# Layer 1's delta-rule scan in a fixed TensorE order: steps of three and six heads, outputs gated straight from PSUM

## The chip, the core and the metric

The kernel runs on one core of one Trainium2 chip. Its time is device microseconds (us) of one execution, the median of several runs. Below, TensorE (PE in the views) does the matmuls and PEld its weight loads, VectorE is DVE, ScalarE is ACT, GpSimd is POOL, and SP issues most DMAs.

## What is computed

A decoder of two layers over 512 tokens of width 1024, in fp32. The first layer mixes tokens with six heads of a gated delta rule, the second with sliding-window attention; both also attend to 256 memory tokens, and both end in a projection `w_out`, a residual add and a SwiGLU block. The change lies in the first layer's scan and what follows it:

```python
def step(state, inp):
    u_n, w_n, a_n, qg_n, kg_n, gl_n = inp
    v_new = u_n - jnp.einsum("bhck,bhkv->bhcv", w_n, state)
    o_n = jnp.einsum("bhck,bhkv->bhcv", qg_n, state) + jnp.einsum("bhcs,bhsv->bhcv", a_n, v_new)
    state = state * gl_n[..., None, None] + jnp.einsum("bhck,bhcv->bhkv", kg_n, v_new)
    return state, o_n
...
o = rms_norm(o, norm_g) * jax.nn.silu(z.reshape(b_sz, s_len, GDN_HEADS, GDN_DV).astype(jnp.float32))
...
x = x + jnp.concatenate([mix_out.astype(x.dtype), mem_o.astype(x.dtype)], axis=-1) @ w_out[layer]
```

## The kernel before, in words

Everything lies feature-major: a tile holds 128 features by 512 tokens. Big products run in fp32r with both operands split into a high and a low part (`mm3`, L205): three matmuls of 128x512 for each 128 features, so a projection (`project`, L213) is 24 of them. A weight arrives by DMA as `wraw` (L183); ScalarE makes its high part `whi` and VectorE its low part `wlo` (`split`, L175). `whi` and `wlo` have three buffers each.

The scan works in chunks of 128 tokens, four for each of the six heads, in plain fp32 products of 128x128. `scan_step` (L726) does one head and one chunk, in five products, called here by what they make:

- the *state* product, from `kn` and the state `S`; VectorE makes `R` of it;
- the *solve* product, from `Tt` and `R`; ScalarE copies it out as `v` (tile `vn`);
- the *keys* product, from `v` and `kg`; VectorE makes the new `S` of it (not in the last chunk);
- the *past* product (`gcr` and the old `S`) and the *own* product (`v` and `DT`), which add up to the chunk's output; ScalarE copies it into `qg` (tile `gcr`).

A head's first chunk has no state: `R` is the value tile itself and the state and past products are left out. All five products of one step lie in one PSUM bank, `sc`, of which there are three; three banks `pj` serve projections and two banks `g` the rest. The value tile (tile `N`) is made from a projection of the input (`conv_tile`, L465: ScalarE's copy, then three taps on VectorE, tile `qv`), a SiLU on ScalarE, four transposes on TensorE into a bank `g`, and one VectorE product.

`gdn` (L475) calls values of heads 0 to 2, their chunks 0 to 2, values of heads 3 to 5, chunk 3 of heads 0 to 2, all chunks of heads 3 to 5, and `finish` (L629), which squares the output, adds the stored square of `q`, sums over features with a matmul by ones (`g<-N,ones`), takes Ln and Exp on ScalarE, multiplies by the norm's gain and by the gate (the stored SiLU of `z`, loaded into `kg`), and splits the result for `output` (L872), whose eight rows of `w_out` each take 24 matmuls. The calls' order is not the order on an engine: a scheduler puts each engine's instructions in an order of its own, within what depends on what, and so mixes products of the scan with those of the value projections and of the first rows of `w_out`. Each engine then runs its list strictly in that order.

## Time and profile before

| | us |
|---|---|
| median of 3 runs (1147.73 to 1148.5) | 1147.86 |
| the profiled execution | 1147.79 |
| its span, first to last instruction | 1146.0 |
| TensorE busy | 1125.1 (98%) |
| VectorE busy | 841.2 (73%) |
| ScalarE busy | 632.8 (55%) |
| mean granted TensorE clock | 0.998 |

Times in the views count from the span's start. An fp32 matmul shows as two records, since it is done in two passes. A matmul's record is longer than the time until the next one can start, so a busy TensorE need not be a TensorE at its peak; start-to-start times tell more. The layer's scan and `finish` lie between about 206 and 280 us.

### The profile page before, as it was taken

What the parts mean: (1) busy time and instruction counts of PE and PEld (TensorE: products, weight loads), DVE (VectorE), ACT (ScalarE), POOL (GpSimd) and SP (SyncE); (2) the same over time, 40 slices, a digit from 0 to 9 for tenths busy, and PEclk for the clock granted to TensorE, in tenths of its full rate; (3) what the DMA queues carried; (4) which work ended last, traced back from release to release, by engine and by line L of the source; (5) the groups of instructions that cost most, each with busy time, mean ns of one, the idle gap of its engine ahead of it and who ended that gap; (6) DMA issues with size and microseconds to landing.
All of it is one profiled execution on the core that took longest, in us unless ns stands there. A gap on an engine that the chain in (4) does not pass through costs nothing.

```text
span 1146.0 us, 19675 instructions
## 1 busy us (share of the span) xinstructions
PE 1125.1 (98%) x7476; PEld 990.9 (86%) x7476; DVE 841.2 (73%) x1591; ACT 632.8 (55%) x1274; POOL 86.0 (8%) x97
## 2 busy tenths in 40 slices
PE   7999999999999999999999999999999999999996
PEld 6888877887899998899998777777999988999986
DVE  6754887766789987489866777859699843898754
ACT  7669572366566652256654556855566522566533
POOL 0310000000101100011100000010011100111000
PEclk9999999999999999999999999999999999999999
DMA  8433342324667744567723411244477733577232
GB/s 310 148 92 115 117 109 96 100 85 166 171 151 187 185 126 126 150 153 188 175 73 102 138 57 56 65 102 129 107 187 187 191 108 106 141 192 185 70 96 93
DMA packets 73971, 152.76 MB, mean 133 GB/s; under 512 B 17756, under 2 KB 18420, under 8 KB 73876
## 3 DMA queue, kind: packets, MB, share of 16 engines
q1 hardware_dynamic: 62356, 130.52, 36.9%
q0 software_dynamic: 11520, 20.98, 11.5%
q8 instruction: 59, 0.97, 0.4%
q14 instruction: 36, 0.29, 0.1%
HBM read 144.51 MB, written 6.96 MB: 132 GB/s over the span
## 4 chain that ended last, share of the span: by engine, by line
PE 84%; DVE 8%; ACT 3%; DMA 2%; issue 1%; SPq 0%; DVEq 0%; ACTq 0%
PE pj L153 39%; PE g L153 37%; PE sc L153 6%; DVE wlo L160 2%; ACT sm L141 2%; ACT whi L147 1%; PE qk L153 1%; DMA wraw<-in_wout 1%; DVE btmp L160 1%; DVE l L163 1%; PE pt L157 1%; DVE big L160 1%; DMA wraw<-in_wmk 1%; PE g L157 1%; DVE stats L791 0%
## 5 line engine op out<-in xcount | busy, mean ns | idle before, releaser
L147 ACT ACTIVATE whi<-wraw 128x512 fp32r<-128x512 f32 (+2 forms) x331 | 244.1, 746 | 238.3 <-PE pj L153 150.5
L160 DVE TENSOR_TENSOR wlo<-wraw,whi 128x512 fp32r<-128x512 f32 (+2 forms) x331 | 274.2, 838 | 100.4 <-ACT whi L147 94.7
L153 PE MATMUL pj<-h,whi 128*128 128x512 f32 (+1 forms) x676 | 265.5, 394 | 0.0
L153 PE MATMUL pj<-l,whi 128*128 128x512 f32 (+1 forms) x676 | 263.9, 390 | 0.4 <-DVE l L163 0.4
L153 PE MATMUL pj<-h,wlo 128*128 128x512 f32 (+1 forms) x676 | 263.6, 390 | 0.0
L153 PE MATMUL g<-T,whi 128*128 128x256 f32 x1280 | 228.1, 278 | 0.2
L153 PEld LDWEIGHTS g<-T,whi 128*128 128x128 f32 x1280 | 194.7, 188 | 1.8 <-DVE fu L163 1.8
L153 PE MATMUL g<-T,wlo 128*128 128x256 f32 x640 | 177.8, 278 | 0.0
L153 PEld LDWEIGHTS pj<-h,whi 128*128 128x128 f32 x676 | 126.8, 188 | 29.0 <-issue 3.3
L153 PEld LDWEIGHTS pj<-h,wlo 128*128 128x128 f32 x676 | 127.0, 188 | 25.9 <-DVE wlo L160 0.4
L153 PEld LDWEIGHTS pj<-l,whi 128*128 128x128 f32 x676 | 127.1, 188 | 25.7 <-DVE l L163 0.8
L153 PE MATMUL g<-h,whi 128*128 128x256 f32 (+1 forms) x508 | 144.4, 284 | 0.0
L153 PE MATMUL g<-h,wlo 128*128 128x256 f32 (+1 forms) x508 | 144.2, 284 | 0.0
L153 PE MATMUL g<-l,whi 128*128 128x256 f32 (+1 forms) x508 | 144.2, 284 | 0.0
L153 PEld LDWEIGHTS g<-T,wlo 128*128 128x128 f32 x640 | 120.1, 188 | 0.0
L153 PEld LDWEIGHTS g<-l,whi 128*128 128x128 f32 x508 | 95.3, 188 | 1.2
L153 PEld LDWEIGHTS g<-h,whi 128*128 128x128 f32 x508 | 95.3, 188 | 1.2
L153 PEld LDWEIGHTS g<-h,wlo 128*128 128x128 f32 x508 | 95.3, 188 | 1.1
L1046 POOL DMA_DIRECT2D ws<-in_wgu x40 | 35.8, 894 | 709.6 <-DMA ws<-in_wgu 313.9
L147 ACT ACTIVATE whi<-ws 128x512 fp32r<-128x512 f32 x80 | 50.5, 631 | 49.0 <-PE g L153 40.1
L160 DVE TENSOR_TENSOR fu<-pj,rstd 128x512 f32<-128x512 f32 (+1 forms) x34 | 22.4, 660 | 54.5 <-PE pj L153 54.5
L160 DVE TENSOR_TENSOR wlo<-ws,whi 128x512 fp32r<-128x512 f32 x80 | 54.9, 686 | 6.4 <-ACT whi L147 6.3
(372 smaller groups left out, 1622.0 us busy)
## 6 DMA issues: line engine op xcount, KB each, us to landing
wraw<-in_wgu SPq DMA_DIRECT2D x48, 512.0 KB, 4.2
ws<-in_wgu SPq DMA_DIRECT2D x80, 256.0 KB, 3.4
ws<-in_wgu POOLq DMA_DIRECT2D x80, 256.0 KB, 4.9
wraw<-in_wdn SPq DMA_DIRECT2D x48, 384.0 KB, 3.1
wraw<-in_win SPq DMA_DIRECT2D x26, 512.0 KB, 3.6
wraw<-in_wgu SPq DMA_DIRECT2D x40, 256.0 KB, 4.5
wraw<-in_wout SPq DMA_DIRECT2D x16, 512.0 KB, 3.5
wraw<-in_wdn SPq DMA_DIRECT2D x16, 256.0 KB, 2.7
```

The source lines that it names most:

```text
L141: ins = self.nc.scalar.activation(out, in_, func, **kw).ins
L147: self.copied = self.nc.scalar.activation(out, in_, AF.Copy, **kw).ins
L153: return self.nc.tensor.matmul(out, lhsT, rhs, start=start, stop=stop, skip_group_check=more).ins
L157: return self.nc.tensor.transpose(out, in_, self.ident[:k, :k]).ins
L160: return eng.tensor_tensor(out=out, in0=a, in1=b, op=op).ins
L163: self.nc.vector.scalar_tensor_tensor(out=out, in0=in0, scalar=scalar, in1=in1, op0=op0, op1=op1)
L1046: nc.gpsimd.dma_start(s1, a22, accum_op=ALU.add)
```

## The change

The scan is rewritten, and TensorE's order in it is fixed: between `lock(True)` and `lock(False)` every matmul and transpose gets an order dependency on the one before it, so that TensorE's list there is the order of the calls. VectorE's and ScalarE's lists are still the scheduler's. In detail:

- Values of heads 0 to 3 are projected first, then heads 0 to 2 are turned and take chunk 0; then come the projections of heads 4 and 5, the turning of heads 3 and 4, chunk 1 of heads 0 to 2, and the turning of head 5.
- Heads 0 to 2 then do chunks 2 and 3 together with chunks 0 and 1 of heads 3 to 5 (six heads in a step); heads 3 to 5 do chunks 2 and 3 by themselves. No other matmul stands inside a step. Between the last two steps stand the sums by ones of heads 0 to 2.
- In a step of three heads the output goes to a bank of its own (`g` or `pj`); in one of six it stays in the step's bank. It is squared by ScalarE from PSUM (into `N`) and multiplied by the gate by VectorE from PSUM (into `gcr`), chunk by chunk. The gates are loaded ahead, into the tiles `big` and `X64`. The copy of the output, the later squares and the later gate products go.
- For heads 3 to 5 the sum by ones takes its input in high and low fp32r parts. Rows 0 to 2 of `w_out` are done k by k, the three rows in turn.

Of the code (line numbers differ between the two kernels):

```diff
+    def chained(self, ins):
+        if self.locked:
+            if self.latest is not None:
+                self.nosync(ins, self.latest)
+            self.latest = ins
+        return ins
...
+        def scan(*steps):
...
+            run("state", todo)
+            if len(groups) > 1:
+                run("solved", todo)
+                for three in groups:
+                    run("keys", three)
+                    for s in three:
+                        s["past"]()
+                        s["own"]()
+                return
+            run("past", todo[:1])
+            run("solved", todo)
+            run("past", todo[1:])
+            run("keys", todo)
+            run("own", todo)
...
-        values(first)
-        scan(first, range(NC - 1))
-        values(second)
-        scan(first, range(NC - 1, NC))
+        self.lock(True)
+        vs += [values(2), values(3)]
+        for h in first:
+            turn(h)
+        scan(*alone(first, 0))
+        vs += [values(4), values(5)]
+        turn(3)
+        turn(4)
+        scan(*alone(first, 1))
+        turn(5)
         self.use(LN_EXP)
-        scan(second)
+        scan(*beside(first, 2, "sc"), *beside(second, 0, "pj"))
+        scan(*beside(first, 3, "sc"), *beside(second, 1, "pj"))
+        squares(first, False)
+        scan(*alone(second, 2))
+        total(first, "pj")
+        scan(*alone(second, 3))
         finish(first)
+        squares(second, True)
...
-        self.mm(ps[:, 2, :], v, AT[:, c, :], S is None, True)
-        self.copy(qg[:, c, :], ps[:, 2, :])
+        def own():
+            self.mm(po, t["v"], AT[:, c, :], old is None, True)
+            self.square(vt[:, c, :], po)
+            self.tt(nc.vector, qg[:, c, :], po, gate[:, c, :], ALU.mult)
```

Three places show what the order becomes; the numbers behind a name tell buffers apart.

**The first chunk.** TensorE before, where heads 0 and 1 start their first chunk (`sc<-N,Tt` is the solve product, `sc<-vn,kg` the keys product, `pj` a value projection):

```order
L157 MATMUL g_2226<-consts_66,qv_2146 128x128 x4
L153 MATMUL sc_2238<-N_572,Tt_1422 128x128
L153 MATMUL pj_2350<-h_456,whi_2346 128x512
L153 MATMUL pj_2350<-l_457,whi_2346 128x512
L153 MATMUL pj_2350<-h_456,wlo_2347 128x512
L153 MATMUL sc_2247<-N_572,Tt_1422 128x128
L153 MATMUL pj_2350<-h_461,whi_2346 128x512
L153 MATMUL pj_2350<-l_462,whi_2346 128x512
L153 MATMUL sc_2238<-vn_2240,kg_131_653 128x128
L153 MATMUL sc_2247<-vn_2249,kg_142_705 128x128
```

TensorE now, the whole first step:

```order
L168 MATMUL g_2265<-consts_66,qv_2109 128x128 x4
L168 MATMUL g_2271<-consts_66,qv_2146 128x128 x4
L168 MATMUL g_2277<-consts_66,qv_2191 128x128 x4
L154 MATMUL sc_2283<-N_572,Tt_1422 128x128
L154 MATMUL sc_2285<-N_572,Tt_1422 128x128
L154 MATMUL sc_2287<-N_572,Tt_1422 128x128
L154 MATMUL sc_2283<-vn_2290,kg_131_653 128x128
L154 MATMUL sc_2285<-vn_2293,kg_142_705 128x128
L154 MATMUL sc_2287<-vn_2296,kg_153_757 128x128
L154 MATMUL g_2284<-DT_112_559,vn_2290 128x128
L154 MATMUL g_2286<-DT_113_560,vn_2293 128x128
L154 MATMUL pj_2288<-DT_114_561,vn_2296 128x128
```

The projections that stood between the products stand ahead of them and behind them. VectorE now, at the same place (`wlo_2742` is the low part of row 0 of `w_out`, `qv_2228` head 3's value):

```order
L171 TENSOR_TENSOR N_572<-g_2265,f_890 128x512
L171 TENSOR_TENSOR N_572<-g_2271,f_890 128x512
L171 TENSOR_TENSOR wlo_2742<-wraw_2739,whi_2741 128x1024
L174 SCALAR_TENSOR_TENSOR qv_2228<-pj_2235,gains_67,qv_2228 128x511
L171 TENSOR_TENSOR N_572<-g_2277,f_890 128x512
```

Head 2's value product stands behind a weight part and a tap.

**The second chunk of heads 0 to 2.** VectorE now (`qv_2353` is head 5's value, three taps; `R` follows the state products):

```order
L171 TENSOR_TENSOR N_572<-g_2390,f_890 128x512
L171 TENSOR_TENSOR N_572<-g_2396,f_890 128x512
L174 SCALAR_TENSOR_TENSOR qv_2353<-pj_2360,gains_67,qv_2353 128x511
L174 SCALAR_TENSOR_TENSOR R_2409<-sc_2402,negc_536,N_572 128x128
L174 SCALAR_TENSOR_TENSOR qv_2353<-pj_2360,gains_67,qv_2353 128x510
L174 SCALAR_TENSOR_TENSOR R_2412<-sc_2404,negc_536,N_572 128x128
L174 SCALAR_TENSOR_TENSOR qv_2353<-pj_2360,gains_67,qv_2353 128x509
L174 SCALAR_TENSOR_TENSOR R_2415<-sc_2406,negc_536,N_572 128x128
L171 TENSOR_TENSOR wlo_2768<-wraw_2765,whi_2767 128x1024
L174 SCALAR_TENSOR_TENSOR S_2430<-S_2299,egl_539,sc_2402 128x128
```

ScalarE at the same place:

```order
L148 ACTIVATE whi_2767<-wraw_2765 128x1024
L148 ACTIVATE qv_2353<-pj_2360,gains_67 128x512
L148 ACTIVATE vn_2419<-sc_2402,f_890 128x128
L148 ACTIVATE vn_2422<-sc_2404,f_890 128x128
L142 ACTIVATE qv_2353<-qv_2353 128x512
L133 ACT_TABLE_LOAD
L148 ACTIVATE vn_2425<-sc_2406,f_890 128x128
```

The three R alternate with the taps of a projection that ends just before; the third `v` stands behind that value's SiLU and the load of the table for Ln and Exp. Before, VectorE alternated R and taps in the same way at one place (R_2474, R_2484, R_2494), with rows of `w_out` between the products on TensorE.

**From the second step of six to chunk 2 of heads 3 to 5.** VectorE now (`gcr<-pj` and `gcr<-sc` are the gate products, `N<-N,kg` the sums of heads 0 to 2):

```order
L174 SCALAR_TENSOR_TENSOR S_2581<-S_2509,egl_539,pj_2529 128x128
L174 SCALAR_TENSOR_TENSOR S_2584<-S_2512,egl_539,pj_2530 128x128
L174 SCALAR_TENSOR_TENSOR S_2587<-S_2515,egl_539,pj_2531 128x128
L171 TENSOR_TENSOR N_572<-N_572,kg_493_2604 128x512
L171 TENSOR_TENSOR gcr_109_550<-pj_2529,big_2183 128x128
L171 TENSOR_TENSOR gcr_110_551<-pj_2530,X_396_2188 128x128
L171 TENSOR_TENSOR N_572<-N_572,kg_494_2607 128x512
L171 TENSOR_TENSOR gcr_111_552<-pj_2531,X_396_2188 128x128
L174 SCALAR_TENSOR_TENSOR R_2617<-sc_2610,negc_536,N_572 128x128
```

The first R of the next step has the gate products and the sums of the step before it in front of it.

184 lines of the change are left out of this document (115 added, 69 removed).

## Prediction

> **What bounds the kernel now.** The page first: busy times, and the chain that ended last by engine.
>
> ```profile
> PE 1125.1 (98%) x7476; PEld 990.9 (86%) x7476; DVE 841.2 (73%) x1591; ACT 632.8 (55%) x1274; POOL 86.0 (8%) x97
> PE 84%; DVE 8%; ACT 3%; DMA 2%; issue 1%; SPq 0%; DVEq 0%; ACTq 0%
> ```
>
> TensorE sets the time, so a microsecond that it waits in the scan is a microsecond of the kernel. Whether it waits there isn't seen in "busy"; it is counted from start-to-start times. The windows by stage for the scan and its finish, whole and for tile `sc` alone, then two groups of that window:
>
> ```profile
> 206.00:280.00 74.00, 72.74 (x413) 59.26 (x412) 50.52 (x92) 42.21 (x92) 0.00 (x0) 1.00 0.37 113
> 206.00:280.00 74.00, 30.50 (x204) 27.58 (x204) 11.34 (x36) 14.13 (x48) 1.00 0.37 113
> L157 PE MATMUL g<-consts,qv 128*128 128x128 f32 x24 | 3.6, 273 | 0.0
> L153 PE MATMUL g<-N,ones 128*128 128x512 f32 x12 | 6.1, 610 | 1.0 <-DVE N L160 1.0
> ```
>
> So 228 records of 128x128 (204 and 24), 12 sums by ones, and 173 others of 128x512. Their spacing, from the chain (72 matmuls), and from the timeline:
>
> ```profile
> 313.00 16.34 PE pj L153 x72
> 219.86 0.53 PEld L153 LDWEIGHTS sc<-S,kn 128*128 128x128 f32 x4
> 220.31 0.19 PEld L153 LDWEIGHTS pj<-h,whi 128*128 128x128 f32 x1
> 251.81 1.02 PE L153 MATMUL g<-N,ones 128*128 128x512 f32 x2
> 252.67 0.38 PE L153 MATMUL sc<-vn,kg 128*128 128x128 f32 x2
> ```
>
> A 128x512 takes 16.34/72 = 0.227 us; four records of 128x128 take 0.45, so 0.1125 each and 0.225 for a scan product; two records by ones take 0.86. The window's work is 173 x 0.227 + 228 x 0.1125 + 6 x 0.86 = 70.1 us of 74: **TensorE waits only 3.9 us there**, because projections stand between the dependent products. That is all that a better order could win.
>
> How long a link of the scan takes, on the timeline of two heads (loads, VectorE, ScalarE, in order of time):
>
> ```profile
> 220.40 0.61 DVE L163 SCALAR_TENSOR_TENSOR R<-sc,negc,N 128x128 f32<-128x128 f32 x2 [0.81 <-PE sc L153]
> 220.81 0.55 PEld L153 LDWEIGHTS sc<-R,Tt 128*128 128x128 f32 x4
> 221.40 0.62 ACT L147 ACTIVATE vn<-sc,f 128x128 f32<-128x128 f32 x2 [0.86 <-PE sc L153]
> 221.82 0.56 PEld L153 LDWEIGHTS sc<-vn,kg 128*128 128x128 f32 x4
> 222.35 0.60 DVE L163 SCALAR_TENSOR_TENSOR S<-S,egl,sc 128x128 f32<-128x128 f32 x2 [0.94 <-PE sc L153]
> 222.75 0.32 PEld L153 LDWEIGHTS sc<-gcr,S 128*128 128x128 f32 x2
> ```
>
> From a product's load to its reader 0.54 (219.86 to 220.40; 0.53 and 0.59 for the others); each R, `v` or S 0.31; from its end to the next load 0.10. So state to solve is 0.95 us, solve to keys 1.01, keys to state 0.93: a ring of 2.9 us, against 15 products x 0.225 = 3.4 us in a step of three heads. By this ring alone such a step has no gap. What decides is whether VectorE and ScalarE start their parts at once; with both lists run strictly in order, that is read from what stands ahead. The durations:
>
> ```profile
> L160 DVE TENSOR_TENSOR wlo<-wraw,whi 128x1024 fp32r<-128x1024 f32 x9 | 11.0, 1217 | 1.7 <-ACT whi L147 1.7
> L147 ACT ACTIVATE whi<-wraw 128x1024 fp32r<-128x1024 f32 x7 | 7.3, 1056 | 4.4 <-PE pj L153 2.4 <-DMA wraw<-in_win 2.0
> L163 DVE SCALAR_TENSOR_TENSOR qv<-pj,gains,qv 128x511 f32<-128x511 f32 x5 | 3.7, 746 | 0.4 <-ACT qv L147 0.4
> L160 DVE TENSOR_TENSOR N<-g,f 128x512 f32<-128x512 f32 x6 | 4.1, 691 | 6.9 <-PE g L157 6.9
> L160 DVE TENSOR_TENSOR N<-N,kn 128x512 f32<-128x512 f32 x6 | 4.0, 688 | 3.4 <-DMA kn<-q 3.4
> L141 ACT ACTIVATE qv<-qv 128x512 f32<-128x512 f32 x6 | 3.8, 627 | 3.7 <-DVE qv L163 3.5
> L132 ACT ACT_TABLE_LOAD x1 | 1.3, 1283 | 0.0
> L147 ACT ACTIVATE gcr<-sc 128x128 f32<-128x128 f32 x24 | 6.5, 275 | 8.8 <-PE sc L153 8.5
> 212.07 0.59 PEld L157 LDWEIGHTS g<-consts,qv 128*128 128x128 f32 x4
> 212.93 0.69 DVE L160 TENSOR_TENSOR N<-g,f 128x512 f32<-128x512 f32 x1 [0.73 <-PE g L157]
> ```
>
> **The change, part by part.** *TensorE's work.* The scan's products are the same. Heads 3 to 5 sum by two fp32r matmuls (0.454) in place of 0.86: 3 x 0.41 = **1.2 us less**.
>
> *Work moved between VectorE and ScalarE.* 24 copies (0.275), six squares and six gate products go; 24 squares and 24 gate products of 128x128 come, three splits too. In sum it costs nothing: the busy sums are 50.5 and 42.2 of 74 us, and VectorE gains about 5 (24 x 0.30 and three splits of 0.69, less six gate products of 0.69). No row shows the new pieces: I take 0.28 for a square (like the copy, the nearest) and 0.30 for a gate product (half of the paired S's 0.60, also two operands, one from PSUM); 0.27 to 0.37 holds both. Nothing is gained on the path, as the copies were off it: no product reads the output. In the new lists VectorE's gate product waits for ScalarE's square of the same bank, so an output is out 0.54 + 0.28 + 0.30 after its own product's load.
>
> *Six gate loads*, ahead of head 4's weights on SP's queue, the first of them waiting for the triangular solve's last reading of `X64`. The rows of the DMA issues (count, size, median us to landing) that bear on this and on the end:
>
> ```profile
> wraw<-in_win SPq DMA_DIRECT2D x26, 512.0 KB, 3.6
> x<-in_xT SPq DMA_DIRECT2D x8, 256.0 KB, 4.1
> kg<-z SPq DMA_DIRECT2D x6, 256.0 KB, 2.9
> ```
>
> Heads 2 and 3 (48 x 0.227 = 10.9 us) are projected meanwhile, so I put it at nothing; were that cover gone, the weight would come 3.6 late, or later by as much as it shares the queues with the gates.
>
> *The first chunk*, time from the end of head 3's projection. A turn's N starts 0.86 after its load (212.07 to 212.93). N0 runs 0.86-1.55, N1 to 2.24; then `wlo` to 3.46 and a tap to 4.20 stand ahead of N2, which ends at 4.89. So head 2's solve product loads at 4.99, its `v` ends at 5.84, its keys product starts at 5.94, and the step's last product ends at 6.8. The work is 12 x 0.1125 + 9 x 0.225 = 3.4: **3.4 us of waiting**.
>
> *The second chunk.* N3 and N4 end at 2.24; tap, R, tap, R, tap, R: the R's end at 3.28, 4.33 and 5.37 where the state products were ready by 2.1. Solve products load at 3.4, 4.4 and 5.5. The third `v` stands behind the SiLU (tap's end 5.07, so to 5.9) and the table load (to 7.2): it ends at 7.5, the keys product follows at 7.6, the step ends at 8.5. Work 0.9 + 15 x 0.225 = 4.3: **4.2 us**. Before, the table load and the taps were there too, with projections to fill the time; now nothing else may pass.
>
> *First step of six.* Head 5's turn needs a bank `g` that the gate product of the step before frees: own product at 7.82, square to 8.64, gate to 8.97, turn at 9.07, N5 to 10.62, then R0, so the first solve product loads at 11.03 in place of 9.6: 1.4. Past and own products share the bank with the keys product here, so they wait until S is read out of it: 0.3 for head 0's and 0.7 in sum for heads 3 to 5's. **2.4 us**.
>
> *Second step of six.* The state products of heads 3 to 5 wait for gate products to free their banks `pj`, and R's run at 0.31 against products at 0.225: the last solve product is 0.5 late. Then head 3's past product waits some 1.0 for S, which stands behind three gate products and a sum (0.69) on VectorE. 27 products are 6.1, and I count 7.5: **1.4 us**.
>
> *Chunk 2 of heads 3 to 5.* Ahead of its R's stand, from the last S, two sums (0.69) and three gate products: 2 x 0.69 + 3 x 0.30 = 2.3. The state product loads 0.8 after that S, and its R could start at 1.35: 0.95 late, and 1.1 with the spacing of the R's: **1.1 us**.
>
> *Chunk 3.* ScalarE's list has three Ln, two Exp and a high part of the first heads ahead of its `v`:
>
> ```profile
> L141 ACT ACTIVATE N<-g,eps 128x512 f32<-128x512 f32 x6 | 4.1, 687 | 1.9 <-PE g L153 1.9
> L147 ACT ACTIVATE h<-gcr 128x512 fp32r<-128x512 f32 x6 | 3.8, 630 | 2.4 <-DVE gcr L160 2.3
> L141 ACT ACTIVATE N<-N 128x512 f32<-128x512 f32 x6 | 3.8, 629 | 0.0
> ```
>
> 3 x 0.69 + 2 x 0.63 + 0.63 = 4.0, from some 1.2 after the first sum loads: 5.2. The first `v` could start when three sums (2.6), three state products and a past one (0.9) and a solve's 0.54 are over, with 0.1 of R: 4.1. **1.1 us**.
>
> *Rows 0 to 2* end together, k by k. Row 3's `whi` waits for row 0's buffer (1.06), its `wlo` (1.22) stands behind two residual adds (0.69 each): about 2.9 after row 1's end against four or five matmuls that can run; and `x` is loaded after the last norm product and lands 4.1 later, which is no later than row 0 is summed. With smaller waits in the second sums: **2.2 us**, from 1 to 3.
>
> Sum: 3.4 + 4.2 + 2.4 + 1.4 + 1.1 + 1.1 + 2.2 = 15.8 us of new waits; less the 3.9 of now, less 1.2 of work: **+10.7 us**. The profiled execution took 1147.79 (span 1146.0 and 1.8 around it; the median is 1147.86): **1158.5 us**.
>
> A rule on the banks bears on the gate products. In the row of 222.75, `sc<-gcr,S` reads the old state alone, yet loads 0.10 after the first S has been read from its bank (222.35 + 0.30): engines take turns at a bank. The Trainium skill ("PSUM — Partial Sum Buffer", PSUM bank collisions raise a hardware error) says that the scheduler does so for any two engines, two readers too. Were square and gate product at once, each boundary would be 0.3 shorter, the sum about 1 us less.
>
> **The rivals.** *Only the first two chunks cost.* If the later steps wait no more than the kernel does now: +3.4 + 4.2 - 1.2 - 2.0 (half of the 3.9, for half of the window) = +4.4: 1152.2. For it: the ring of 2.9 in a step of 3.4. Against it: the gate products ahead of the R's.
>
> *Faster: the ring decides.* If N2 and the R's come in time, no step has a gap and TensorE gets back all: -3.9 - 1.2 = 1142.7; it decides where the R's stand at most 0.5 us behind their state products (3.4 less 2.9). For it: 98% busy and VectorE at 50.5 of 74. Against it: the lists above, with a `wlo` and three taps in front.
>
> *A slower clock after the waits.* At the start, after 7 us with nothing to do, TensorE takes nearly twice as long for a 128x256 (the waits' row, then four matmuls):
>
> ```profile
> PE pj L153 <- ACT whi L147: 7.1, 1, 7.1
> 10.72 0.41 PE L153 MATMUL pj<-mh,whi 128*128 128x256 f32 x1
> 10.93 0.41 PE L153 MATMUL pj<-ml,whi 128*128 128x256 f32 x1
> 11.90 0.28 PE L153 MATMUL pj<-ml,whi 128*128 128x256 f32 x1
> 12.02 0.28 PE L153 MATMUL pj<-mh,wlo 128*128 128x256 f32 x1
> ```
>
> That is 0.21 apart, then 0.12; the change comes some 4 us after the wait's end. The first step holds one wait of 2.7 us (from 2.3 to 4.99), the second four of 0.8 to 1.5. If such waits slow TensorE for as long as the start did, each of the two steps adds 2: 1162.5. Against it: shorter, and the window's clock is 1.00 with waits in it. The Trainium skill ("TensorE: Matmul & The Clock Gate", Why this matters for your kernels) asks for no idle gaps over about 3 us; by it the wait just passes. *Nothing happens*: 1147.8, if the new waits are a third of what I count.
>
> **How the numbers follow.** Forecast 0.65; first chunks alone 0.15; slower clock 0.07; faster 0.08; no change 0.05. The likeliest: 1158.5. Its own ends are 1154 (no tail, and half of what I count from the first step of six on) and 1162.5 (pieces of 0.37, a tail of 3, S and R at 0.35 as singles). With the second case, 1151 to 1163 holds about 0.8. Slower by over 0.2% (2.3 us, about what a measurement of this kernel can tell) 0.87, within 0.05, faster 0.08.
>
> **What would show it.** Right: between the projections of heads 3 and 4 some 6.8 us in place of 3.4, `N<-g` behind `wlo` at its end; R's spaced 1.05 in the second step, `vn` behind the table load; the scan and its finish some 10 us longer, all else the same. Wrong: steps of three that take 3.4 us from first to last load, or a `wlo` that has long run when N1 ends.

## The result, and the profile after

The change makes the kernel slower: 1155.28 us, the median of 6 executions from 1154.77 to 1157.57, against 1147.8 for the kernel before, measured beside it. The ratio is 1.0071 [1.0058, 1.0084], or +7.5 us. A second set, taken later, gave 1156.77 against 1147.55, 1.0074 [1.006, 1.0087], +9.2. The forecast was 1158.5, +10.7: slower, as forecast, and by waits of the kind that were forecast, but 3.2 less than that.

The page of the kernel after, busy times and the chain by engine:

```profile
PE 1127.3 (98%) x7476; PEld 994.8 (86%) x7476; DVE 844.3 (73%) x1612; ACT 631.6 (55%) x1271; POOL 86.3 (7%) x97
PE 88%; DVE 6%; ACT 3%; DMA 1%; issue 1%; SPq 0%; DVEq 0%; ACTq 0%
```

The profiled execution took 1155.4 with a span of 1153.6, 7.6 more than before. TensorE's share of the chain rises from 84 to 88% and VectorE's falls from 8 to 6, while the scan holds more waits: the chain's shares do not show where the time goes. The busy sum does not either; at a halved clock a matmul also counts as busy for longer.

The windows by stage, over the same stretch as before (PE, PEld, DVE, ACT, POOL busy, the granted clock, the DMAs):

```profile
206.00:280.00 74.00, 67.69 (x384) 57.38 (x383) 50.12 (x108) 37.67 (x85) 0.00 (x0) 0.98 0.25 81
```

TensorE has 384 records in place of 413 there, is idle for 6.3 us in place of 1.3, and its clock is 0.98 in place of 1.00. Two things, then: waits, and a slower clock. What TensorE waited for between 190 and 300 us (total, times, longest):

```profile
PE sc L154 <- DVE R L174: 2.6, 5, 1.0
PE sc L154 <- DVE N L171: 1.2, 1, 1.2
PE g L168 <- ACT qv L142: 1.0, 1, 1.0
PE sc L154 <- ACT vn L148: 0.9, 1, 0.9
PE pj L154 <- DVE S L174: 0.4, 1, 0.4
PE g L168 <- DVE gcr L171: 0.2, 1, 0.2
```

And the same view of the kernel before, from 200 to 290 us:

```profile
PE g L153 <- DVE N L160: 1.0, 1, 1.0
PE sc L153 <- ACT gcr L147: 0.3, 1, 0.3
```

The waits are 6.3 us against 1.3. They are on the tiles that the forecast named, `N`, `R`, `v` (tile `vn`), `S` and, for turn 5, the gate products (`gcr`); only `qv`, a SiLU, is new. The first step's place, on the timeline after:

```profile
216.45 1.03 PEld L168 LDWEIGHTS g<-consts,qv 128*128 128x128 f32 x8
216.68 1.03 PE L168 MATMUL g<-consts,qv 128*128 128x128 f32 x8
218.52 1.22 DVE L171 TENSOR_TENSOR wlo<-wraw,whi 128x1024 fp32r<-128x1024 f32 x1
218.75 0.66 PE L168 MATMUL g<-consts,qv 128*128 128x128 f32 x4 [1.04 <-ACT qv L142]
219.66 0.74 DVE L174 SCALAR_TENSOR_TENSOR qv<-pj,gains,qv 128x511 f32<-128x511 f32 x1
220.32 0.68 DVE L171 TENSOR_TENSOR N<-g,f 128x512 f32<-128x512 f32 x1
221.05 0.65 PE L154 MATMUL sc<-N,Tt 128*128 128x128 f32 x2 [1.20 <-DVE N L171]
222.78 1.06 PE L154 MATMUL g<-DT,vn 128*128 128x128 f32 x4
223.92 0.77 PE L154 MATMUL pj<-h,whi 128*128 128x512 f32 x1
```

From the first turn to head 4's projection are 7.24 us, of which 3.4 is work. Head 2's turn waits for its SiLU; its `N` stands behind `wlo` and a tap as forecast; and four records of an own product then take 1.06 where four took 0.61 elsewhere (the row of 242.53, the same product in the second chunk). That is the clock, for 3.4 us, in the windows of the last section.

The second chunk, where the list on VectorE alternates taps and R's, and ScalarE has the table load:

```profile
235.25 1.04 PE L168 MATMUL g<-consts,qv 128*128 128x128 f32 x8
238.15 0.49 PE L154 MATMUL sc<-R,Tt 128*128 128x128 f32 x2 [0.97 <-DVE R L174]
239.06 0.49 PE L154 MATMUL sc<-R,Tt 128*128 128x128 f32 x2 [0.42 <-DVE R L174]
240.49 1.28 ACT L133 ACT_TABLE_LOAD   x1
241.79 0.37 ACT L148 ACTIVATE vn<-sc,f 128x128 f32<-128x128 f32 x1
242.21 0.49 PE L154 MATMUL sc<-vn,kg 128*128 128x128 f32 x2 [0.85 <-ACT vn L148]
242.53 0.61 PE L154 MATMUL g<-DT,vn 128*128 128x128 f32 x4
243.62 0.66 PE L168 MATMUL g<-consts,qv 128*128 128x128 f32 x4 [0.25 <-DVE gcr L171]
```

Solve products 0.91 apart (forecast 1.05), the third `v` right behind the 1.28 us table load, then turn 5 held until a gate product has freed its bank. From the first turn's start to the last product's end (243.2) the step takes 8.0, where 8.5 was forecast; turn 5 starts 8.4 after the first turn, where 9.07 was.

One wait outside the scan was in no sum. Where the feed-forward block begins, after:

```profile
313.20 0.39 PE L154 MATMUL pj<-h,wlo 128*128 128x512 f32 x1
314.02 0.68 DVE L171 TENSOR_TENSOR x<-pj,x 128x512 f32<-128x512 f32 x1
314.85 0.47 PE L154 MATMUL pj<-h,whi 128*128 128x512 f32 x1 [1.25 <-DVE x L171]
```

And before:

```profile
307.53 0.69 DVE L160 TENSOR_TENSOR x<-pj,x 128x512 f32<-128x512 f32 x1
307.62 0.39 PE L153 MATMUL pj<-h,whi 128*128 128x512 f32 x1
```

Before, matmuls go on there, at 307.40 and 307.62, while VectorE reads the last row's sum from 307.53 on. After, the next matmul starts 0.15 after that reading has ended, 1.65 after the one before it, so 1.42 is lost. The two kernels have the same code there, but the program gives row 7's sum and the block's first product the same bank, while before they had different ones: the rotation over the banks `pj` is shifted by the tiles the new scan takes from it.

The difference by place. TensorE's lists of the two kernels, and of every kernel below, are the same up to one matmul of head 2's projection, called the *shared matmul* here: it starts at 207.94 before and at 207.38 after, so this execution was 0.56 ahead there, by chance: the change's second one, of which more below, was 1.23 behind. From it to row 3's residual add (285.38 and 292.32), the first mark past the scan, are 77.45 us before and 84.95 after, 7.50 more; to row 7's add (307.53 and 314.02) 99.59 and 106.64, 7.05 more. The 0.45 between is work: two matmuls of row 4 now stand ahead of row 3's add. At the block's start 1.42 is added, and from the shared matmul to the end 8.2 is left (938.1 and 946.3 us). The 0.56 taken off, that is the 7.6 between the spans.

### The profile page after: what moved, and what is told of

Same layout as the page of the kernel before. It is cut to its first block, busy times and chain, and to the rows that moved or that the text cites. A ratio compares the mean times of both kernels' runs of the same rounds, so it can differ in the third digit from the quotient of the medians.

```text
span 1153.6 us, 19690 instructions
## 1 busy us (share of the span) xinstructions
PE 1127.3 (98%) x7476; PEld 994.8 (86%) x7476; DVE 844.3 (73%) x1612; ACT 631.6 (55%) x1271; POOL 86.3 (7%) x97
## 4 chain that ended last, share of the span: by engine, by line
PE 88%; DVE 6%; ACT 3%; DMA 1%; issue 1%; SPq 0%; DVEq 0%; ACTq 0%
PE pj L154 43%; PE g L154 37%; PE sc L154 6%; DVE wlo L171 2%; ACT sm L142 1%; ACT whi L148 1%; PE qk L154 1%; DVE l L174 1%; DMA wraw<-in_wout 1%; PE g L168 1%; PE pt L168 1%; DVE fu L174 1%; DMA wraw<-in_wmk 1%; DVE T L171 0%; DVE sqa L171 0%
```

## The experiments

Every kernel was timed beside the kernel before. Medians in us; the last column is from one trace of each, the time from the shared matmul to the end over the 938.1 of the kernel before, with a star where TensorE's clock was halved for a time ahead of the kernel's end (the change itself: +8.2*):

| what | this | before | ratio | in the trace |
|---|---|---|---|---|
| turn 2 inside head 4's projection | 1154.19 | 1147.12 | 1.006 [1.0047, 1.0074] | +5.8 |
| waits filled with matmuls | 1155.37 | 1147.12 | 1.0071 [1.0058, 1.0083] | +6.9 |
| table load later | 1154.73 | 1147.12 | 1.0066 [1.0054, 1.0079] | +7.4* |
| no fixed order | 1151.68 | 1147.12 | 1.0038 [1.0025, 1.005] | +3.8 |
| row 4 in another bank | 1154.42 | 1146.97 | 1.0066 [1.0054, 1.0079] | +5.9 |
| chunks inside projections | 1151.65 | 1146.97 | 1.0041 [1.0027, 1.0054] | +3.9 |
| before, with fp32r sums | 1146.75 | 1146.97 | 0.9999 [0.999, 1.0008] | -1.1 |
| outputs copied first | 1157.34 | 1146.97 | 1.0091 [1.0077, 1.0104] | +8.4* |
| new pieces, order of before | 1150.61 | 1147.55 | 1.0023 [1.0014, 1.0032] | +3.7* |
| chunks inside projections, 2nd | 1151.37 | 1147.55 | 1.0034 [1.0022, 1.0047] | +3.6 |
| chunks inside projections, 3rd | 1149.49 | 1146.72 | 1.0025 [1.0016, 1.0034] | +1.4 |
| the change again | 1156.77 | 1147.55 | 1.0074 [1.006, 1.0087] | +8.2* |

The theory: in a fixed order without other matmuls inside a step, TensorE waits for whatever stands ahead of `N`, `R` and `v` on VectorE and ScalarE. The rivals: the new pieces cost (gating from PSUM, the splits of the sums); or the clock that slows after the waits does.

**Is it the fixed order?** The first kernel takes away the lock alone and leaves the rest of the change.

```diff
-        self.lock(True)
```

> The changed kernel without the lock: the calls stay as they are, but the scheduler may put TensorE's list in an order of its own. Its list still holds no projection and no row of w_out between the first and the last product of any step, since the banks for them are taken; it only mixes products of neighbouring steps. Theory (the cost comes from what stands near the scan, not from the order being fixed): the same waits in the first two chunks, 0.5 to 1.5 us less in the steps of six: 1153.5 to 1155. Rival (the fixed order itself costs): the 3.9 us of waiting of the kernel before and 1.2 less work: 1146.6 to 1149.

It came out at +4.6 in place of +7.5 in the change's first set: the lock itself costs about 3, between what the two theories had. Its waits, in the stretch up to the feed-forward block:

```profile
PE pj L154 <- DVE x L171: 1.3, 1, 1.3
PE sc L154 <- ACT vn L148: 1.1, 4, 0.5
PE sc L154 <- DVE N L171: 1.1, 2, 0.8
PE pj L154 <- DVE S L174: 0.7, 1, 0.7
PE pj L154 <- ACT Y L148: 0.5, 1, 0.5
```

The waits for R are gone, since the scheduler puts products of the neighbouring steps there; no projection and no row of `w_out` stands in the first two chunks. What is left is 3.4 in the scan, where before had 1.3, and the bank's 1.3. In this trace row 7's add comes 2.4 later than before, counted from the shared matmul (102.01 in place of 99.59), and the bank's 1.4 behind it. So the calls and the pieces cost without the lock too.

**Do the single waits cost what they seem to?** Heads 3 and 4 are projected ahead of chunk 0, with head 2's turn inside head 4's projection:

```diff
-        vs += [values(2), values(3)]
-        for h in first:
-            turn(h)
+        vs.append(values(2))
+        turn(0)
+        turn(1)
+        vs.append(values(3))
+        vs.append(values(4, {2: [lambda: turn(2)]}))
...
-        vs += [values(4), values(5)]
+        vs.append(values(5))
```

> One edit to the changed kernel: heads 3 and 4 are projected ahead of the first chunk, head 2 is turned inside head 4's projection, and only head 5 is projected after the chunk. In the changed kernel's trace the first chunk loses 4.3 us: a wait of 1.20 for head 2's SiLU, one of 1.36 for N2, and 1.7 in which products are spaced 0.21 instead of 0.11 at a granted clock of 0.53. Theory (the first chunk costs because its values are late): both waits go and with them the slow clock; 0.3 for the ring of solve and keys and 0.3 for head 4's copy ahead of the first v are left: 3.7 us faster than the changed kernel, about 1151.6. Rival (a wait moves elsewhere: another value or a bank is late instead): at most 1 us faster, 1154.3 or more. Rival (the slow clock is not caused by the waits): the waits go and the slow clock stays, 2 us faster, 1153.3.

+7.1: by the median almost nothing came back, where 3.7 had been expected. The timeline of this kernel, at the first step:

```profile
224.06 1.06 ACT L148 ACTIVATE whi<-wraw 128x1024 fp32r<-128x1024 f32 x1 [1.15 <-PE pj L154]
225.60 0.88 ACT L148 ACTIVATE vn<-sc,f 128x128 f32<-128x128 f32 x3
226.01 1.00 PE L154 MATMUL sc<-vn,kg 128*128 128x128 f32 x6 [1.08 <-ACT vn L148]
```

The waits for the SiLU and for `N` are gone, but the projection that was moved ahead of the step ends right before it, so the next weight's high part (1.06) and the projection's copy stand ahead of `v` on ScalarE: a wait of 1.08 takes the place of two. In the trace row 3's add still comes 2.8 earlier than with the change, counted from the shared matmul (82.14 in place of 84.95), but there was no slow clock in that stretch either. The run with row 4 in another bank (below) has the change's own scan, and its trace no slow clock: 83.61. So 1.5 is what this edit gave.

The table load is moved behind the `v` of chunk 2 of heads 3 to 5:

```diff
-        self.use(LN_EXP)
...
         scan(*alone(second, 2))
+        self.use(LN_EXP, self.copied)
```

> The changed kernel with the load of the table for Ln and Exp moved: it follows the last v of chunk 2 of heads 3 to 5 and so runs beside the sums by ones. In the second chunk of heads 0 to 2 the third v no longer stands behind it. The changed kernel's trace has a wait of 1.01 for that v. Theory (each of the terms in the second chunk is a wait of its own): 1.0 us faster, 1154.3. Rival (the wait is hidden behind the next one, the turn of head 5, which waits for a gate product): 0.0 to 0.4 faster, 1155. Rival (the load is in the way at its new place too: squares and Ln later): 0, or up to 0.5 slower.

In its trace the wait of the third `v` is gone, and turn 5 starts 4.35 after the first solve product of its chunk (238.26 to 242.61) in place of 5.47 (238.15 to 243.62): 1.1, as expected. At row 7's add the 1.1 is still there (105.54 from the shared matmul in place of 106.64, both with the slow clock in the first chunk). The median is at +7.6: an effect of 1 us is not seen through differences from execution to execution that are as large.

**Is it the clock?** Ten matmuls of 128x512, whose result nobody reads, are put into the two waits of the first chunk, so that TensorE has work while it waits.

```diff
...
+        filler = self.bank("pj")
+        warm = lambda n: [self.mm(filler, self.onesr, mq[0][0]) for _ in range(n)]
+        warm(5)
+        turn(2)
+        scan(*alone(first, 0), before_last=lambda: warm(5))
```

> The changed kernel with idle work added: five 128x512 matmuls, whose result nobody reads, ahead of the turn of head 2, and five more ahead of the third solve product of the first chunk, 10 x 0.227 = 2.3 us of work in two waits of 1.20 and 1.36. Nothing else changes. Theory (the clock falls because TensorE worked too little in the 3.4 us before): the granted clock stays at 1.00 and the chunk's products are 0.11 apart: 1.7 us faster than the changed kernel although there is more to do, about 1153.6. Rival (the clock falls for another reason, or at the same time in each run): 0.5 is granted again, 1155.3; if the fillers also delay the turn, up to 1156.

By the windows of its trace, TensorE is busy for 3.42 us from 217.66 to 221.08 and for 3.27 of the 3.41 us behind, the clock stays at 1.00, and from the first turn to row 3's add are 74.27 us in place of 75.64: 1.37 shorter, where 1.7 was expected if too little work lets the clock fall. The median, at +8.3, shows none of it. In three of its five executions the mean clock of the whole was 0.995 or 0.996, below the 0.997 and 0.998 of the kernel before beside it, so the clock seems to have fallen in them, at a place that no trace shows. (The mean also counts a half clock behind the last matmul, from 1149.66 on in the change's trace; so 0.997 by itself tells nothing.) To see whether the place belongs to the order of the instructions, the change was run again, unaltered.

> The changed kernel itself, once more, beside the same runs of the kernel before as the two others. Theory (the clock is halved in the first two chunks in some executions and not in others, by where a window of 3.4 us falls): 7 to 9 us over the kernel before, in an execution without it about 1.5 us less than in one with it; the waits of 1.20 and 1.36, 1.13, 0.59, 0.59 and 1.01, and the 1.42 at the start of the feed-forward block are there again, within 0.3. Rival (the slow clock belongs to the order of the instructions): it is granted at the same place, between 221 and 225 us, in each trace.

It does not. In this trace the halved clock is in the second chunk, from 240.97 to 244.38, and the first chunk, with the same waits, has the full clock. The slower clock is a real part of the cost, but only part, and it moves. It is worth 0.9 to 1.4 us a time: 1.37 above, and from the shared matmul to row 3's add the change's two traces have 84.95 and 84.54, the one with row 4 in another bank, without a slow clock, 83.61.

**The bank.** Row 4 of `w_out` takes its sum in a bank `g`, which shifts the rotation of `pj` by one.

```diff
-        if m % 3 < 2:
+        if m % 3 < 2 and (m != 4 or self.pbufs["pj"] < 3):
```

> The changed kernel with one row of w_out in another bank: row 4 is summed in a bank g in place of a bank pj, so that the rows after it take the banks pj one place earlier in their turn. The changed kernel's trace has a wait of 1.42 us at 313 us, at the first matmul of the feed-forward block: it writes the bank in which row 7 of w_out was summed and waits until VectorE's residual add has read it; the trace of the kernel before has no wait there. Theory (the change shifted the turn of the banks, and that costs 1.4 us outside the scan): the wait goes, nothing else changes, 1.4 us faster than the changed kernel: 1153.9 beside a kernel before of 1147.8, that is 6.1 over it. Rival (the first gate of the block waits for the last high and low part h, l in any case, 0.7 to 1.4 after the add): 0 to 0.3 faster. Rival (row 4 in bank g makes row 5 wait for it): as much lost as won.

In the trace TensorE has no wait at the block's start, and from row 3's add to a mark past it (the residual add at 444.80 in the change's trace) are 150.99 us in place of 152.48: 1.49 less. The median's +7.5 does not show it. That the bank is the cause is shown by the trace of this run; what it is worth at the end of the kernel is not settled by its median.

**Do the pieces cost?** Three kernels. Outputs are copied to SBUF first, and squared and gated from there:

```diff
-            self.square(vt[:, c, :], po)
-            self.tt(nc.vector, qg[:, c, :], po, gate[:, c, :], ALU.mult)
+            self.copy(qg[:, c, :], po)
+            self.square(vt[:, c, :], qg[:, c, :])
+            self.tt(nc.vector, qg[:, c, :], qg[:, c, :], gate[:, c, :], ALU.mult)
```

> The changed kernel with the outputs taken out of PSUM as before: ScalarE copies an output to SBUF, and square and gate product read the copy; the order on TensorE is the same. A bank is free after the copy, 0.54 + 0.28 after the own product's load, in place of 0.54 + 0.28 + 0.30. Theory (the gate product that waits for the square holds the banks): the turn of head 5 waits 0.1 in place of 0.41, the waits of 0.16 and 0.10 for banks go, and the R's of chunk 2 may pass the gate products: 0.5 to 1 us faster than the changed kernel, 6.5 to 7 over the kernel before. Rival (24 more pieces of 0.28 on ScalarE stand in front of its v): 0.5 to 2 us slower, 8 to 9.5 over it. Rival (neither is on the path): no change, 7.5 over it.

+10.4, but at a mean clock of 0.996 in all four executions, which were at 1156.81 to 1158.4; the change's own four at that clock were at 1155.15 to 1157.26. In the trace, with one fall of the clock as in the change's, row 7's add comes 106.71 us after the shared matmul, where the change's two traces have 106.64 and 106.28. So without gating straight from PSUM nothing comes back, and these runs don't show that it gains anything either; 24 copies on ScalarE come in its place here, so its own price is not separated.

The kernel before, with fp32r sums for all six heads, and nothing else:

```diff
-                self.mm(ps, self.ones, sq)
+                two = [self.t(gp, [P, T], F32R, f"DT{h}"), self.t(gp, [P, T], F32R, "qv", 5)]
+                self.split(sq, *two)
+                for i in range(2):
+                    self.mm(ps, self.onesr, two[i], i == 0, i == 1)
```

> The kernel before with one part of the change alone, taken for all heads: the sums by ones of its six heads take their input in high and low fp32r parts, two matmuls of 0.227 in place of 0.86. Theory (TensorE sets the time there): 6 x 0.41 = 2.4 us less work. The split adds 0.63 on ScalarE and 0.69 on VectorE ahead of each sum; for heads 0 to 2 rows of w_out and the scan stand beside it, for the last heads only rows of w_out that are left: 0 to 1 us of that shows. So 1.4 to 2.4 us faster than the kernel before. Rival (the split is in the chain of the last heads, whose sum the kernel before already waits 1.15 us for): 3 x 1.3 more, slower by 1 to 2. Rival (the sums are hidden): no change.

No change, 0.9999. TensorE has 2.4 us less to do, and two more instructions, the split, stand between a square and its sum. In the trace row 7's add comes 0.8 earlier, counted from the shared matmul (98.78 in place of 99.59); the median has none of it.

Then all new pieces (turns, squares and gates from PSUM, fp32r sums), called in the old order, without the lock:

```diff
...
+        made(first)
+        each(first, range(NC - 1))
+        made(second)
+        each(first, range(NC - 1, NC))
...
+        each(second)
+        for heads, exact in ((first, False), (second, True)):
+            for h in heads:
+                squares([h], exact)
+                total([h], "g")
+                finish([h])
```

> The changed kernel's new pieces in the order of the kernel before: outputs are squared and gated straight from PSUM (in the step's own bank sc), gates are loaded ahead, and heads 3 to 5 are summed in fp32r parts; but the calls for values, turns, steps of one head, sums, finish and rows of w_out come as in the kernel before, and TensorE's list is the scheduler's again. Theory (the order costs, the pieces don't): TensorE has 1.2 us less to do than in the kernel before and waits as much as there: 0 to 1.5 us faster than the kernel before. Rival (the pieces cost: the gate product behind the square holds the bank of a step 0.3 longer, and VectorE has 24 pieces of 0.29 more): the next step's state product waits for a bank, 1 to 3 us slower than the kernel before.

+3.1: that the pieces, called like this, cost nothing is wrong. The rival's waits for a bank do not show; its timeline shows what costs, at the sums:

```profile
269.27 1.31 PE L154 MATMUL g<-DT,ones 128*128 128x512 f32 x2 [1.96 <-ACT DT L148]
```

Sums wait 1.96 us for the high part on ScalarE; called at the end of the scan, there is little else to do, and two windows at half the clock follow (last section). In its four executions with the highest mean clock (0.997 to 0.998) it was at 1149.4 on average, +1.9, about this wait.

**Can the order be mended?** Chunks 0 and 1 are put inside the projections of heads 4 and 5, stage by stage, between groups of projection matmuls; the bank and the table load are as in the runs above.

```diff
...
+        do = lambda *names: lambda: now[0](*names)
+        vs.append(values(4, {1: [lambda: turn(2), lambda: begin(0)], 4: [do("state", "solved")], 6: [do("keys")], 7: [do("own")]}))
+        vs.append(values(5, {0: [lambda: turn(3)], 1: [lambda: begin(1), do("state")], 3: [do("solved")],
+                             5: [do("past", "keys")], 6: [do("own")]}))
```

> The changed kernel with the order changed and still fixed: chunk 0 of heads 0 to 2 lies inside head 4's projection and chunk 1 inside head 5's, a few products after each 6 to 9 matmuls of the projection, so that each link of 1.0 us has 1.4 us of other work beside it; chunk 2 of heads 0 to 2 is a step of three ahead of head 5's turn, chunk 3 goes with chunk 0 of heads 3 to 5, and those do three steps alone. The table load follows the v of chunk 2 of heads 3 to 5, and row 4 of w_out is summed in a bank g. Nothing is left out. In the changed kernel's trace the first chunk loses 4.3 us with the slow clock and the second 3.9. Theory (these are waits for links that had no other work beside them): both go; head 5's taps are now ahead of the R's of chunk 2, 2.3, and its turn waits for its SiLU, 1; a sixth step alone costs 0.6 more; the bank gives 1.4: 1155.3 - 8.2 + 3.9 - 1.4 = 1149.6, that is 1.8 over the kernel before. Rival (waits move from place to place, VectorE's and ScalarE's lists being the limit): 1152 or more, 4 over the kernel before.

+4.7: about 3 less than the change, but more than the +1.8 expected. R's still wait (2.2 in five waits), turns wait for gate products (1.5), and the bank's wait was back, since the new order shifts the rotation once more. A second try moves the stages to later groups and brings chunk 2 and the turn of head 4 in as well:

```diff
...
+        vs.append(values(4, {3: [lambda: turn(2), lambda: begin(0)], 5: [do("state", "solved")], 7: [do("keys")]}))
+        vs.append(values(5, {0: [do("own"), lambda: turn(3)], 1: [lambda: begin(1), do("state")], 2: [do("solved")],
+                             4: [do("past", "keys")], 5: [do("own")], 6: [lambda: turn(4)], 7: [lambda: begin(2)]}))
```

> The woven order again, still fixed, with what its first try showed mended: head 2 is turned two thirds of a microsecond twice later inside head 4's projection (it waited 1.18 for its SiLU), head 4 is turned inside head 5's projection, so that the R's of chunk 2 stand ahead of head 5's taps (they lost 1.6 behind them), head 5 is turned between the solve and the past products of the last chunk of heads 0 to 2 (0.65), and the banks pj are taken 12 times ahead of w_out in place of 13, so that row 7 does not end in the bank that the feed-forward block begins with (1.42). The first try lost 8.1 + 1.4 us to waits in the scan and behind it and took 4.7 over the kernel before. Theory (every wait is a link without other work beside it, and can be given some): 1.18 + 1.3 + 0.5 + 1.42 less: 0.3 over the kernel before, between 0.7 under and 1.5 over. Rival (waits only move): 3 or more over it.

+3.8, with the bank's wait still there (this time the expectation had the rotation miscounted) and turn 3 held 1.0 by a gate product that stands behind two taps. A third has turn 3, the own products and the sums of heads 0 to 2 elsewhere:

```diff
...
+        vs.append(values(4, {2: [lambda: turn(2), lambda: begin(0)], 4: [do("state", "solved")], 5: [do("keys")], 6: [do("own")]}))
+        vs.append(values(5, {1: [lambda: turn(3), lambda: begin(1), do("state")], 2: [do("solved")],
+                             4: [do("past", "keys")], 5: [do("own")], 6: [lambda: turn(4)], 7: [lambda: begin(2)]}))
```

> The second woven order with three edits, still fixed. Chunk 0 of heads 0 to 2 is one sixth earlier inside head 4's projection and head 3 is turned one sixth later inside head 5's: in the second try that turn waited 1.0 to 1.2 for its bank g, which a gate product behind two taps on VectorE still held. The sums of the squares of heads 0 to 2 follow their next step in place of standing ahead of its R (0.84 there). And the order in which banks pj come free is another, so that row 7 of w_out is summed in a bank other than the one in which the feed-forward block begins: in the programs that block always begins in bank 0, row 7 lies in bank 0 in the changed kernel and in both woven tries, where 1.42 us are waited, in bank 1 in the kernel before and in the try with row 4 moved, where nothing is waited, and in bank 2 here. Theory (banks and links): 1.42 + 1.1 + 0.4 less than the second try's 3.8 over the kernel before: about 0.9 over it, between 0 and 2; no wait at the start of the feed-forward block. Rival (the wait at that start is for the high and low parts, not for the bank): it is there again, 2.3 over. Rival (waits only move): 3 or more over it.

+2.8, the best of the fixed orders and still slower than before. What TensorE waited for in it, to the feed-forward block:

```profile
PE sc L156 <- DVE R L176: 2.0, 3, 1.2
PE sc L156 <- DVE S L176: 0.6, 2, 0.4
```

The bank's wait and the turn's are gone; chunk 1's R's are behind taps now. The three orders by hand are 4.7, 3.8 and 2.8 slower than before, each with a wait in a new place; the best does about what the scheduler does with the same pieces in the order of before (+3.1). No version was faster than the kernel before.

## Why the prediction was right or wrong

**What failed.** Its steps for the scan, as waits in us, foreseen and measured (time between the starts in the trace, less the work at the prediction's 0.225 for a product and 0.1125 for a turn's transpose):

| step | foreseen | measured |
|---|---|---|
| first chunk | 3.4 | 3.9 |
| second chunk, to its last product | 4.2 | 3.7 |
| first step of six, with the hold of turn 5 | 2.4 | 1.8 |
| second step of six | 1.4 | 1.0 |
| chunk 2 of heads 3 to 5 | 1.1 | 0.7 |
| chunk 3 | 1.1 | 0.45 |
| rows 0 to 2 | 2.2 | 0.6 |
| sum | 15.8 | 12.1 |

With 0.4 more, where head 4's first matmuls still run at the slow clock, and 0.2 in small ones it is 12.7. The same comes out as a whole: 84.95 us from the shared matmul to row 3's add, less 72.3 of work at the prediction's prices. Before had 4.4 of waits there (77.45 less 73.0), where 3.9 was counted up to 280, and the work falls by 1.2 as forecast: 12.7 - 4.4 - 1.2 = 7.1, and row 7's add is 7.05 later, counted from the shared matmul. To it comes the bank's 1.42; some 0.3 is given back later, and 0.56 is what this execution was ahead by at the shared matmul: 7.6, the difference of the spans. In the forecast's terms: 10.7, less 3.1 of waits that were not there, less 0.5 of the old waits under-counted, plus 1.4, less 0.9, is 7.6; the medians say 7.5. That the two lie so close is partly luck, as the 0.56 is not the change's.

**The terms that were mis-sized** are the later ones. "Rows 0 to 2 end together" cost 0.6 in place of 2.2, chunk 3 0.45 in place of 1.1, and the first step of six 1.8 in place of 2.4. One reason is in the way that lists were added up. Rows of the timeline after:

```profile
255.66 0.48 DVE L171 TENSOR_TENSOR gcr<-sc,big 128x128 f32<-128x128 f32 x2
261.99 2.74 PE L154 MATMUL pj<-N,ones 128*128 128x512 f32 x6
263.11 0.69 ACT L142 ACTIVATE N<-pj,eps 128x512 f32<-128x512 f32 x1 [0.64 <-PE pj L154]
264.37 1.25 ACT L142 ACTIVATE N<-pj,eps 128x512 f32<-128x512 f32 x2
266.54 0.88 ACT L148 ACTIVATE vn<-sc,f 128x128 f32<-128x128 f32 x3
```

Two Ln back to back take 1.25, not 2 x 0.69; two gate products 0.48, not 2 x 0.29 (the single row below); three `v` 0.88, not 3 x 0.31. A list that is summed from single durations is too long, the more instructions it has: chunk 3's `v` starts 4.55 after the first sum (261.99 to 266.54), where 5.2 had been counted. At the tail, rows 0 to 2, the timeline after has

```profile
286.96 0.19 PEld L154 LDWEIGHTS pj<-mq0h,wlo 128*128 128x128 f32 x1 [0.43 <-DVE wlo L171]
```

The low part of row 3's weight is late, as foreseen, but it ends 2.0 after row 1's end (286.91 and 284.88), where 2.9 had been counted. The high part is in time: row 3's first two matmuls follow row 2 without a gap (285.56 and 285.79). Two matmuls of row 4 (286.24 and 286.58, the first held for its own high part) fill most of the rest. The five matmuls from 285.56 to 287.31 take 1.75 where 1.13 is work: 0.6, not 2.2.

The lower end that the forecast named, 1154, is a slip of its sum: without the tail's 2.2 and half of the 6.0 from the first step of six on, 1158.5 becomes 1153.3. The range on record, 1151 to 1163, takes in a rival below that and does not hang on it.

**What held.** The first two chunks, 7.6 foreseen for both and about as much measured: `N` behind `wlo` and a tap, R's between taps, `v` behind the table load, each on the named engine. The new pieces: no row had shown them, 0.28 and 0.30 were taken, and it was

```profile
248.40 0.28 ACT L151 ACTIVATE N<-sc 128x128 f32<-128x128 f32 x1 [0.84 <-PE sc L154]
248.71 0.29 DVE L171 TENSOR_TENSOR gcr<-sc,big 128x128 f32<-128x128 f32 x1 [0.60 <-ACT N L151]
```

The gate product starts 0.03 after the square has ended, as the rule on banks had it that was weighed there (the Trainium skill, "PSUM — Partial Sum Buffer", PSUM bank collisions raise a hardware error): the scheduler makes two readers of a bank take turns, and the rows agree.

But the first chunk's agreement, 3.4 and 3.9, is partly luck. `N` ended 4.55 after the first turn's load (216.45 to 221.00), where 4.89 had been counted; by the same steps from there 3.1 of waiting were left. The other 0.8, and the 0.4 in head 4's matmuls, is the clock, which had been a rival at 0.07; the run with filled waits gained 1.37 by keeping the full clock. The wait for head 2's SiLU was not foreseen, and lengthened nothing, as its `N` stood behind `wlo` anyway.

**"All else the same"** failed: a bank's turn past the scan cost 1.42. The change moved no instruction there. It could have been read blind, as the program gives out the banks before it runs.

**The rivals.** "Only the first two chunks cost", +4.4, is refuted by the 4.5 of waits in the steps behind them, where it left 1.9, the other half of the 3.9. "Faster" and "nothing" are refuted by the medians. The slower clock is there, but with some 1.3 in one step of the trace, not 2 in each of two, and not in every execution.

**What stays open.** The parts as found are the lock (2.9 by medians; 3.3 in traces without a slow clock, as row 7's add comes 105.35 us after the shared matmul with it, in the run with row 4 in another bank, and 102.01 without it), the bank (1.4 in a trace), the clock (0.9 to 1.4 a time), and waits that are left without the lock (3.4, of which before had 1.3). They overlap, since the waits are what lets the clock fall, and the small ones were each seen in traces and not in medians.

The unaltered change gave +7.5 once and +9.2 once. Its two profiled executions, 1155.4 and 1157.26, each had one fall of the clock, and from the shared matmul to the end they agree: 946.25 and 946.32 us, +8.2 both times. The 1.8 between them lies ahead of that matmul (207.38 and 209.17), where no instruction differs. Why that stretch differs between executions, and whether it is also what parts the two medians, is not known.

## What to carry to other kernels

Where independent matmuls stand between dependent ones, a fixed order that takes them out costs what every other list has queued ahead of the link, and mending one link uncovers the next: count the waits that there are (4.4 us here) before you buy them off. After any change in a rotation of banks, look at the first product of the block behind it. An effect below the spread from execution to execution is read between two marks of a trace, the first of them right ahead of the change, with the clock beside it, and its price at the end is claimed only when the median has it.

## What the hardware showed

The granted clock is set in windows of 3.413 us on a grid that runs freely of the program: in the change's trace 208.213 us at the full clock, 61 such windows, are followed by 3.413 at half of it, and a window ends 13.9 us after the shared matmul there (221.24), but 11.3 and 14.7 us after it in the second trace. The windows of the change's trace, then of its second run, then of the kernel with the new pieces in the old order (columns as above; PE's busy time and the clock matter):

```profile
217.82:221.24 3.42, 1.29 (x9) 1.10 (x10) 3.42 (x6) 2.08 (x5) 0.00 (x0) 1.00 0.39 105
221.24:224.65 3.41, 3.41 (x16) 3.31 (x16) 2.37 (x8) 1.27 (x5) 0.00 (x0) 0.50 0.34 131
```

```profile
237.55:240.97 3.42, 1.60 (x9) 1.12 (x9) 3.42 (x8) 1.26 (x4) 0.00 (x0) 1.00 0.00 0
240.97:244.38 3.41, 3.22 (x16) 2.93 (x14) 1.73 (x5) 1.94 (x4) 0.00 (x0) 0.50 0.48 148
```

```profile
265.31:268.73 3.42, 1.62 (x7) 0.68 (x5) 2.29 (x6) 2.32 (x6) 0.00 (x0) 1.00 0.01 2
268.73:272.14 3.41, 2.87 (x7) 2.15 (x8) 2.56 (x4) 2.59 (x5) 0.00 (x0) 0.50 0.00 0
272.14:275.55 3.41, 3.41 (x10) 2.64 (x9) 2.50 (x4) 2.65 (x5) 0.00 (x0) 0.50 0.04 9
```

A window in which TensorE was busy for 1.29 of 3.42 us (0.38), 1.60 (0.47) or 1.62 (0.47) is followed by one at half the clock. The third of the hand orders had one at 1.82 of 3.41 (0.53), and the window behind it kept the full clock:

```profile
228.40:231.81 3.41, 1.82 (x12) 1.15 (x10) 3.41 (x8) 0.36 (x2) 0.00 (x0) 1.00 0.48 154
```

In all 14 traces, no full-clock window of 0.53 or more was followed by a fall, and each of 0.47 or less was. A half-clock window that was full (3.41, 3.22) brought the clock back; after one of 2.87 a second followed. Ahead of the kernel's end, where TensorE has nothing left to do, no single wait in the windows that led to a fall was longer than 2.0 us. The Trainium skill ("TensorE: Matmul & The Clock Gate", Why this matters for your kernels) asks for no idle gaps over about 3 us; these rows differ from it, as several short waits in one window do the same.

A fall cost 0.9 to 1.4 us in the change's scan. A second window costs about as much again, by an estimate: from 272.14 to 275.55 eight matmuls are 0.43 apart in place of 0.23, which is 1.6. Whether a fall comes depends on where the grid lies over the waits: the first chunk, with the same waits, was busy for 0.38 of one window in the change's first trace and for 0.71 and 0.63 of two in its second. Of the change's 11 executions the four with a mean clock of 0.998 or more were at 1154.77 to 1155.62, the seven others at 1155.15 to 1157.57. So waits of a few us on TensorE add a price that differs from execution to execution. Together with the differences ahead of the scan, that hid the 1 us effects above.
